# Loading three image pairs in one transfer each instead of two halves, in a sparse 3x3 convolution

## The chip, the cores and the metric

The kernel runs on one core of a Trainium2 chip. The metric is the device time of one execution in microseconds (us). Beside it stands the profile of one execution: its span runs from the first to the last instruction of the program, and it is a little shorter than the device time.

## The reference

The kernel computes a 3x3 convolution with zero padding of 1 over 16 images of 64 channels and 64x64 pixels, into 128 channels. Nine tenths of the weight's entries are zero, at random places; the kernel computes it densely.

```python
def reference(x, weight):          # x (16, 64, 64, 64), weight (128, 64, 3, 3), float32
    x_pad = np.pad(x, ((0, 0), (0, 0), (pad, pad), (pad, pad)), mode='constant')
    output = np.zeros((batch, c_out, h, w), dtype=np.float32)
    ...
                        if weight[co, ci, kh, kw] != 0:
                            output[b, co] += weight[co, ci, kh, kw] * x_pad[b, ci, kh:kh+h, kw:kw+w]
```

Input x is 16.8 MB, the output 33.6 MB, both float32 in HBM.

## The kernel before, in words

Two images make a pair: 2 x 64 channels fill the 128 partitions. There are eight pairs, p = 0 to 7. Each pair is worked on in four blocks of 16 output rows, so there are N = 32 blocks, k = 0 to 31, and block k belongs to pair k // 4. "The sixth, seventh and eighth pair" are p = 5, 6 and 7, and they are first used in blocks 20, 24 and 28.

For two output rows at a time the three row taps are folded into three products (five groups of matmuls, where plain work would take six). For each block GpSimd (POOL) makes `sums` (even rows plus odd rows, line 181) and `even` (a copy of the even rows, line 170), and ScalarE (ACT) makes `odd` (a copy of the odd rows, line 161). TensorE (PE) runs 30 matmuls on them (line 321). ACT copies the first product out of PSUM (line 276), and VectorE (DVE) adds it to the other two (lines 289 and 293) and so writes the output rows in SBUF. `sums`, `even` and `odd` have two buffers each, so POOL may be up to two blocks ahead: before it fills buffers for block k it waits until PE has done the products of block k-2 that read them (line 267).

Transfers go by two queues. SyncE's queue (SP, hardware descriptors, "q1 hardware_dynamic") loads the weight and the upper half of pair 0, and stores the output: pairs 0 to 5 in one transfer of 4 MB each (line 306), pairs 6 and 7 in two halves of 2 MB, the last half at line 355. A store is asked for when DVE has written its last row (a wait on `s_out`), and DVE may write an output buffer again four pairs later, once its store has landed (line 286). POOL's queue (software descriptors, "q0 software_dynamic") loads the images and casts them from float32 to bfloat16 on the way (line 103, in `load`): 1 MB are read and 0.5 MB written for a whole pair. Both queues feed the same 16 DMA engines.

When a load is asked for stands in two tables written out by hand. `PIECES[p]` (lines 39 to 43) lists the row ranges in which pair p is loaded; each piece has its own semaphore. `WHEN` (line 44) says behind which block's fills POOL asks for which piece. Pairs 0 to 3 are asked for before the loop over the blocks. Pair 4 comes in two pieces of 28 and 36 rows behind blocks 1 and 6. The loop on POOL is

```python
    for k in range(1, N):
        for fill_in, product in ((fill_sums, 2), (fill_even, 6)):
            if k >= UNROLL:
                wait(g, s_pe, 6 * (k - UNROLL) + product)
            fill_in(k)
        if k in WHEN:
            load(*WHEN[k])
```

A fill waits for every piece that holds one of its rows (`source`, lines 119 to 124). With halves, blocks 20, 24 and 28 need only the first half of their pair, and the next block already needs the second, since `even` reads one row beyond its 16.

Of the kernel before, what the change touches and what calls it, by code (L numbers as in the profile page):

```python
# [22 lines left out]
def kernel(  # L23
# [7 lines left out]
    B, C_IN, H, W = x.shape  # L31
# [7 lines left out]
    PIECES = {p: [(0, H)] for p in range(NP)}  # L39
    PIECES[0] = [(HEAD, H)]  # L40
    PIECES[4] = [(0, 28), (28, H)]
    for p in (5, 6, 7):
        PIECES[p] = [(0, H // 2), (H // 2, H)]
    WHEN = {1: (4, 0), 6: (4, 1), 8: (5, 0), 11: (5, 1), 14: (6, 0), 17: (6, 1), 20: (7, 0), 24: (7, 1)}

    def sbuf(name, shape, dtype):
        return nc.alloc_sbuf_tensor(name, shape, dtype).ap()
# [53 lines left out]
    def load(p, i=0):  # L101
        a, b = PIECES[p][i]
        nc.gpsimd.dma_start(out=xs[p][:, a:b, :], in_=pair(p)[:, a:b, :]).then_inc(s_x[p][i], 16)  # L103
# [160 lines left out]
# [8 lines that stand above are left out]
# [9 lines left out]
    for k in range(N):  # L281
        p, b = divmod(k, BLOCKS)
# [110 lines left out]
```

## Time and profile before

| | us |
|---|---|
| median of 3 runs | 126.63 |
| the runs | 125.82, 126.63, 131.43 |
| the profiled execution, its own device time | 126.62 |
| span of the profiled execution | 124.8 |
| PE busy in it | 110.0 |
| POOL busy in it | 64.3 |
| all 16 DMA engines together: packet time of both queues | 97.9% of the span |

The median and the profiled execution agree, so the profile stands for the median. Busy time of an engine counts its computing instructions; a DMA packet is one contiguous piece that one of the 16 DMA engines moves, and the share of a queue is the time of all its packets divided by 16 spans. Packets of one engine overlap slightly in the records, so a share of 102% in a stretch means full.

### The profile page before, as it was taken

The page shows a single profiled execution, that of the slowest core. Times are in us where ns is not written, and L with a number is a line of the kernel's source. Part 1 is how long each engine was busy: PE and PEld are TensorE (multiplying, and loading weights), DVE is VectorE, ACT ScalarE, POOL GpSimd, SP SyncE. Part 2 cuts the span into 40 slices and gives each one's busy share as a digit, 9 for nine tenths or more (in the row PEclk, how much of TensorE's full clock was granted, in tenths as well). Part 3 has the DMA queues.
Part 4 walks back from the last instruction along what each step waited for, and adds up shares of the span by engine and source line. Part 5 has one row for each costly group of instructions (what it writes and reads, how often), then busy time and mean ns, then how long its engine had stood idle before and what let it go on. Part 6 is the DMA issues. An engine that isn't in the chain of part 4 may idle for free.

```text
span 124.8 us, 2486 instructions
## 1 busy us (share of the span) xinstructions
PE 110.0 (88%) x983; PEld 56.5 (45%) x983; DVE 82.6 (66%) x74; ACT 54.5 (44%) x78; POOL 64.3 (52%) x89
## 2 busy tenths in 40 slices
PE   5979999999999999999999999999999999990000
PEld 1435555555555555555555555555555555540000
DVE  0576777777777777777777777777777777773000
ACT  4524555555555555554444444444444555530000
POOL 4469555575755755755675575557555555100000
PEclk9999999999999999999999999999999999999555
DMA  3999999999999999999999999999999999999990
GB/s 109 350 219 221 215 218 213 191 429 407 342 330 285 390 410 356 338 427 349 374 370 345 364 432 345 341 416 420 352 339 428 431 407 428 423 428 428 426 391 32
DMA packets 4739, 42.79 MB, mean 343 GB/s; under 512 B 384, under 2 KB 384, under 8 KB 1664
## 3 DMA queue, kind: packets, MB, share of 16 engines
q1 hardware_dynamic: 3008, 34.90, 66.9%
q0 software_dynamic: 1728, 7.87, 31.0%
q14 instruction: 3, 0.02, 0.0%
HBM read 17.07 MB, written 33.55 MB: 406 GB/s over the span
## 4 chain that ended last, share of the span: by engine, by line
PE 82%; DVE 2%; issue 0%; DVEq 0%
PE ps L321 82%; DVE home L293 1%; DVE home L289 1%; DVEq L144 0%
## 5 line engine op out<-in xcount | busy, mean ns | idle before, releaser
L276 ACT COPY pc<-ps 128x1024 f32<-128x1024 f32 x32 | 32.4, 1012 | 51.9 <-PE ps L321 51.9
L321 PE MATMUL ps<-odd,wT 64*128 64x504 bf16 (+1 forms) x384 | 47.2, 377 | 0.0
L321 PE MATMUL ps<-even,wT 64*128 64x504 bf16 (+1 forms) x384 | 47.2, 377 | 0.0
L289 DVE TENSOR_TENSOR o<-ps,pc 128x1024 f32<-128x1024 f32 x24 | 29.4, 1225 | 19.6 <-PE ps L321 19.6
L321 PEld LDWEIGHTS ps<-even,wT 64*128 64x128 bf16 x384 | 21.6, 94 | 19.9
L321 PEld LDWEIGHTS ps<-odd,wT 64*128 64x128 bf16 x384 | 21.6, 94 | 19.9
L293 DVE TENSOR_TENSOR o<-ps,pc 128x1024 f32<-128x1024 f32 x24 | 29.4, 1225 | 0.0
L321 PE MATMUL ps<-sums,wT 64*128 64x504 bf16 (+1 forms) x192 | 26.5, 377 | 0.7 <-PEq L332 0.7
L181 POOL TENSOR_TENSOR sums<-x 128x512 bf16<-128x512 bf16 x20 | 23.1, 1154 | 0.1
L170 POOL COPY even<-x 128x576 bf16<-128x576 bf16 (+1 forms) x20 | 13.0, 650 | 19.2 <-PE ps L321 19.2
L321 PEld LDWEIGHTS ps<-sums,wT 64*128 64x128 bf16 x192 | 10.7, 94 | 10.9 <-issue 1.2
L181 POOL TENSOR_TENSOR sums<-home 128x512 bf16<-128x512 bf16 (+1 forms) x11 | 13.3, 1212 | 2.8 <-DMA home<-in_x_dram 2.8
L289 DVE TENSOR_TENSOR home<-ps,pc 128x1024 f32<-128x1024 f32 x8 | 9.8, 1225 | 6.3 <-PE ps L321 6.3
L161 ACT COPY odd<-x 128x576 bf16<-128x576 bf16 (+1 forms) x20 | 13.2, 660 | 0.0
L170 POOL COPY even<-home 128x576 bf16<-128x576 bf16 (+2 forms) x11 | 6.7, 609 | 8.2 <-PE ps L321 8.0
L293 DVE TENSOR_TENSOR home<-ps,pc 128x1024 f32<-128x1024 f32 x8 | 9.8, 1225 | 0.0
L161 ACT COPY odd<-home 128x576 bf16<-128x576 bf16 (+1 forms) x10 | 6.6, 657 | 0.0
L171 POOL MEMSET even<- 128x64 bf16 x8 | 1.2, 151 | 10.3 <-PE ps L321 10.3
L237 PE MATMUL ps<-idle_rhs 128*128 128x512 bf16 x14 | 5.3, 538 | 1.4 <-DVE idle_rhs L202 1.4
L103 POOL DMA_DIRECT2D x<-in_x_dram x9 | 5.1, 565 | 0.0
L237 PEld LDWEIGHTS ps<-idle_rhs 128*128 128x128 bf16 x14 | 1.7, 129 | 3.7 <-issue 1.9
L198 DVE CAST w_bf<-w_sb 128x192 bf16<-128x192 f32 (+1 forms) x4 | 1.1, 352 | 2.4 <-DMA w_sb<-in_weight_dram 2.4
(21 smaller groups left out, 15.2 us busy)
## 6 DMA issues: line engine op xcount, KB each, us to landing
out_dram<-o SPq DMA_DIRECT2D x5, 4096.0 KB, 18.4
out_dram<-home SPq DMA_DIRECT2D x1, 4096.0 KB, 19.1
out_dram<-o SPq DMA_DIRECT2D x2, 2048.0 KB, 14.4
out_dram<-home SPq DMA_DIRECT2D x2, 2048.0 KB, 11.1
x<-in_x_dram POOLq DMA_DIRECT2D x6, 512.0 KB, 13.1
home<-in_x_dram POOLq DMA_DIRECT2D x2, 1024.0 KB, 13.5
home<-in_x_dram SPq DMA_DIRECT2D x1, 1024.0 KB, 5.9
x<-in_x_dram POOLq DMA_DIRECT2D x1, 1024.0 KB, 20.0
```

Of the source, the lines that this page charges most:

```text
L103: nc.gpsimd.dma_start(out=xs[p][:, a:b, :], in_=pair(p)[:, a:b, :]).then_inc(s_x[p][i], 16)
L161: copy or (lambda o, i: nc.scalar.copy(out=o, in_=i)),
L170: copy or (lambda o, i: nc.gpsimd.tensor_copy(out=o, in_=i)),
L171: zero or (lambda o: nc.gpsimd.memset(o, 0.0)),
L181: engine.tensor_tensor(out=sums[k % UNROLL], in0=src[:, r0 : r0 + ROWS : 2, :], in1=src[:, r0 + 1 : r0 + ROWS : 2, :], op=ADD,).then_inc(s ...
L198: copy(out=w_bf4[:, g, a:b, :], in_=w_v[:, k : k + b - a, :]).then_inc(done, 1)
L237: t.matmul(idle_ps, idle_rhs[:, 0:128], idle_rhs, start=True, stop=True)
L276: a.copy(out=pc[k % 3], in_=ps[0]).then_inc(s_pc, 1)
L289: v.tensor_tensor(out=o[:, :, r0 : r0 + ROWS : 2, :], in0=ps[1], in1=pc[k % 3], op=ADD).then_inc(s_free, 1)
L293: v.tensor_tensor(out=o[:, :, r0 + 1 : r0 + ROWS : 2, :], in0=ps[2 + k % 2], in1=pc[k % 3], op=ADD).then_inc(s_out, 1)
L321: mm = t.matmul(into[:, n, :, c_lo:c_hi], tap(g, kw, n), src[q, i : i + HALF, c_lo + kw - 1 : c_hi + kw - 1], start=(m == 0), stop=(m == l ...
```

## The change

```diff
     PIECES[4] = [(0, 28), (28, H)]
-    for p in (5, 6, 7):
-        PIECES[p] = [(0, H // 2), (H // 2, H)]
-    WHEN = {1: (4, 0), 6: (4, 1), 8: (5, 0), 11: (5, 1), 14: (6, 0), 17: (6, 1), 20: (7, 0), 24: (7, 1)}
+    WHEN = {1: (4, 0), 6: (4, 1), 8: (5, 0), 14: (6, 0), 21: (7, 0)}
```

Pairs 5, 6 and 7 keep the piece list that all pairs start with, `[(0, H)]`: one transfer with one semaphore. Pair 5 is asked for behind block 8 (its halves: blocks 8 and 11), pair 6 behind block 14 (14 and 17), pair 7 behind block 21 (20 and 24). The order of all computing instructions, and the stores, stay as they are. POOL issues three DMA instructions fewer, 9 instead of 12.

## The prediction

> **What bounds the kernel now.** I read the page first, then the chain of waits, then the table by stretches, then POOL's timeline. The page:
>
> ```profile
> PE 110.0 (88%) x983; PEld 56.5 (45%) x983; DVE 82.6 (66%) x74; ACT 54.5 (44%) x78; POOL 64.3 (52%) x89
> PE   5979999999999999999999999999999999990000
> DMA  3999999999999999999999999999999999999990
> DMA packets 4739, 42.79 MB, mean 343 GB/s; under 512 B 384, under 2 KB 384, under 8 KB 1664
> q1 hardware_dynamic: 3008, 34.90, 66.9%
> q0 software_dynamic: 1728, 7.87, 31.0%
> ```
>
> Two resources are full for nearly the whole span: PE until about 113 us, and the DMA engines from 3 us to the end. The two queues' packets fill 66.9 + 31.0 = 97.9% of 16 engines' span, 122.2 of 124.8 us. The chain of waits (start, length, what) names PE, but look where it ends:
>
> ```profile
> 8.28 102.64 PE ps L321 x948
> ...
> 112.24 1.23 DVE home L293
> ```
>
> DVE's last row is written at 113.47 us. The other 11.3 us of the span are the last store: SP's timeline has it (line 355) asked for at 113.76, and its 2 MB are 256 packets of 8 KB, 16 for each DMA engine at 309 ns (the trace's record of DMA packets), 4.9 us in all. So it waits and moves for 10.2 us (its time to landing) what takes 4.9. The table by stretches says why (stretch, length, PE, PEld, DVE, ACT, POOL busy, PE's clock, DMA share, GB/s):
>
> ```profile
> 48.00:60.00 12.00, 12.00 (x115) 6.27 (x112) 8.83 (x8) 6.42 (x9) 7.22 (x10) 1.00 1.02 369
> 72.00:84.00 12.00, 12.00 (x114) 6.28 (x112) 9.48 (x8) 5.45 (x8) 6.84 (x10) 1.00 1.03 386
> 108.00:114.00 6.00, 4.19 (x40) 1.93 (x35) 4.67 (x4) 1.01 (x1) 0.00 (x0) 1.00 1.01 427
> 114.00:118.00 4.00, 0.00 (x0) 0.00 (x0) 0.00 (x0) 0.00 (x0) 0.00 (x0) 0.69 1.01 426
> 118.00:122.00 4.00, 0.00 (x0) 0.00 (x0) 0.00 (x0) 0.00 (x0) 0.00 (x0) 0.50 0.88 371
> ```
>
> The DMA share is 1.00 or more in each stretch from 4 to 118 us. The last store queues behind earlier stores; its first packet moves at 116.7. **The DMA engines set the end, and they have no idle time before it**: the end comes when the sum of all packets is through, whatever their order. One engine finishes late, at 123.6, where the middle one of the 16 finishes at 121.7; the span ends on that one.
>
> How near is PE's path? The first store is asked for at 22.73 and its first packet moves at 25.0, 2.3 us later, with no store ahead of it. The last store could thus start at 113.76 + 2.3 = 116.1 instead of 116.7 (0.6 us of slack), and on the late engine, which starts it at 123.6 - 4.9 = 118.7, 2.6 us earlier. That is the most that the DMA work ahead can give; beyond it PE's pace (3.24 us a block) sets the end.
>
> **The change part by part.** *Packets removed.* Each half moves 128 packets that write 4096 bytes, one for each partition; a whole pair moves 128 of 8192. The packet records have 625 ns for the 8192-byte load packets (384 of them, pairs 1 to 3) and 324 ns for the 4096-byte ones (896, nearly all beside stores; median 322). Each transfer ends with 16 packets of 4 bytes, about 16 ns each. Before: 768 x 324.5 = 249.2 us of engine time for pairs 5 to 7; after: 384 x 625.2 = 240.1. Difference 9.1 / 16 = 0.57 us, and 48 closing packets fewer, 48 x 16 / 16 = 0.05 us. Sum: 0.62 us less DMA time. With the median of 322 for the small ones it is 0.45 + 0.05 = 0.50.
>
> Bounds: in a stretch in which only whole loads run, shares above 100% show that consecutive load packets overlap, so part of the cost of a packet may be hidden already. Two answers on the DMA queues, of 12:22 and of 46:54 us (packets, MB, share):
>
> ```profile
> q0 software_dynamic: 294, 2.15, 102.8%
> ```
>
> ```profile
> q1 hardware_dynamic: 159, 2.36, 70.1%
> q0 software_dynamic: 143, 0.52, 32.4%
> ```
>
> In the first, the 2.8% above full are 4.5 us over 262 load packets, 17 ns of overlap for each. In the second, with halves beside stores, the 2.5% are 3.2 us over some 128 load packets, up to 25 ns for each if all of it is theirs. The overlap is thus about as large as the 19 to 24 ns by which a packet is dearer, and if it came with every packet, small or large, the gain would be 0. Between 0 and 0.62 I take 0.5, near the packet times: store packets overlap too, so part of the second's 25 ns is theirs. Packet times and overlaps allow no more than 0.62, and a loss only if 8192-byte packets run slower beside stores than alone, which no row shows.
>
> *Closing cost of a transfer.* The Trainium skill (DMA: Bandwidth & Descriptors, "Anatomy of one DMA — SWDGE (gpsimd) path") puts about 2.0 us of fixed cost on each software-descriptor DMA; three fewer would give 6 us by that figure, as an estimate. The row speaks against it here: with other packets queued, the engines read 1.02 and 1.03 through the stretches in which halves close, so the fixed time is latency of one transfer and not idle engines.
>
> *Instructions on POOL.* DMA issues at blocks 11, 17, 20 and 24 go, one at 21 comes, 567 ns each: three fewer, 1.7 us of POOL time. POOL has idle time beside them (it waits 27.2 + 10.3 us for PE before `even`, 1.42 us in a block without an issue, 0.88 in one with), so this is worth nothing. The one added issue, at block 21, delays `sums` of block 22 from 74.03 to 74.6; the `even` behind it waits for PE until 76.61 anyway, and PE reads those sums some 5 us later. If that cover were gone, the cost would be 0.57 us. ACT and DVE issue nothing else; SP's queue is not touched, its stores are asked for at DVE's pace.
>
> *New waits.* Block 28 now needs all of pair 7, block 24 all of 6, block 20 all of 5. POOL's timeline (start, length, what):
>
> ```profile
> 73.37 0.66 POOL L170 COPY even<-x 128x576 bf16<-128x576 bf16 x1 [0.88 <-PE ps L321]
> ...
> 80.52 1.15 POOL L181 TENSOR_TENSOR sums<-x 128x512 bf16<-128x512 bf16 x1
> ...
> 93.48 1.15 POOL L181 TENSOR_TENSOR sums<-x 128x512 bf16<-128x512 bf16 x1
> ```
>
> The first row is `even` of block 21, so pair 7 is asked for at 74.03; the others are `sums` of blocks 24 and 28. Pair 7 must land by 93.48 for POOL not to wait, 19.4 us on. Behind that wait on POOL stand `even` of 28 and all later fills; PE reads `sums` of 28 at 99.04, so PE would wait only if the pair lands after 99.04 - 1.17 = 97.9, 23.8 us on (ACT's `odd` of 28 starts at 97.6). How long does a whole pair take beside stores? No row shows it. From below: a half takes 12.6 to 13.8 us. From above: pair 3, the one whole load behind two others, took 20.0, landing at 94.0, 0.5 late for POOL and early for PE. Between: a half's first packet moves 3.7 to 4.9 us after the issue, and its 8 packets per engine alternate with 16 KB store packets, 8 x (0.324 + 0.62) = 7.6 us, 12.3 of the 13.3 measured. Whole: 4.7 + 8 x (0.625 + 0.62) + 0.8 = 15.5 us. I take this; it lands at 89.5, 4 us before POOL's date. Cost 0. Pair 6 is asked for at 51.3 for 80.5, pair 5 at 31.8 for 67.5: 29 and 36 us ahead.
>
> *Order of DMA work.* The second halves of 5 and 6 move up by about 10 us, the first of 7 back by 3.3. Moving up only adds to the queue. Moving back could starve the engines at 71 to 76 us; but the store of pair 3 (asked for at 61.6, landing in 19.1 us) is still moving then, with about 5 us of packets left at 74, and pair 4's store is asked for at 74.6. So no idle time arises. Stores may land a few us later than now; pair 3's is asked for at 61.6, lands at 80.7, and DVE needs its buffer at block 28, after 99.0.
>
> Sum against the profiled execution: 126.62 - 0.5 = **126.1 us**; the 1.8 us outside the span stay. The median of the three runs, 126.63, is that execution's time.
>
> **The rivals.**
>
> *Packets already overlap.* All of the 19 to 24 ns of a packet is hidden, so nothing is gained: 126.6. For it: the 17 to 25 ns above. Against it: part of that overlap is that of store packets.
>
> *Slower: the whole pair 7 lands too late.* Place: POOL's wait ahead of `sums` of block 28. It decides from a landing of 97.9 on for PE, and for the end from 97.9 + 2.6 = 100.5 on, since the last store has that slack on the late engine. It would take engines that serve stores first: at 74 the store of 3 has 5 us left, that of 4 takes 256 x 611 ns / 16 = 9.8, that of 5 (asked for at 87.6) another 9.8, and then the pair 5.0: landing at 103.6. PE would be 103.6 + 1.2 - 99.0 = 5.8 late, the last store would start at 116.1 + 5.8 = 121.9 and end by 126.8, the span some 3 us later: 129.8. Against it: in 46:54 above both queues move at once, 70 to 32, and no load beside a store took over 13.8 us except the first piece of pair 4, queued behind others at 17.1. The Trainium skill (the same page, "Queues, rings and completion order") has the engines go round the queues packet by packet, which that row agrees with.
>
> *Faster than the packets say: a fixed cost of each transfer comes off the engines.* Three transfers at any cost over 0.9 us each would run into PE's path: at most 2.6 us, 124.0. Nothing in the stretches shows such idle time. The skill's 2.0 us, above, is the rule that would give it.
>
> *The change does nothing to the transfers*, because packets stay 4096 bytes: excluded nearly, since pairs 1 to 3 are loaded by the same call and have 8192.
>
> **How the numbers follow.** Forecast (0.3 to 0.9 us gained) 0.58; no gain, to within 0.3, 0.27; late pair 7, 0.05, of which a part costs under 2%; fixed cost comes off, 0.03; some other shift of a microsecond in the order of packets or in which engine ends last, 0.07. Runs of the same kernel differ by 0.8 us (125.82 and 126.63), and 2% (2.5 us) is about what a measurement of this kernel can tell from no change. The forecast's own range is 125.7 to 126.4; with the no-gain case and the scatter between runs it is 125.2 to 127.2. Faster by over 2%: 0.02; within 2%: 0.94; slower: 0.04.
>
> **What would show it.** Right: q0 with 1728 - 384 - 48 = 1296 packets and its share at (38.7 - 0.6) / 124.3 = 30.7%; packets under 8 KB down to 848; DMA share still 1.00 or more in all stretches from 4 to 118 us; PE without a new wait in front of blocks 20, 24, 28; whole loads landing in 15 to 17 us; DVE's last row still at 113.5, and the last store landing in about 9.7 us instead of 10.2. Wrong: a wait of POOL on pair 7 longer than 4 us, a stretch in the middle with a DMA share under 1, a whole load beside stores over 20 us, or load packets of 8192 bytes dearer than 644 ns beside stores: then the gain is a loss of as many ns x 24.

## The result, and the profile after

The changed kernel takes 126.65 us (median of 21 runs, 126.43 to 133.06), the kernel before 126.05 us beside it (21 runs, 125.75 to 131.95). The ratio is 1.0053, with a 95% interval of 1.004 to 1.0066; it leaves out the few executions of either kernel that took over 1.5% more than its fastest. The changed kernel is thus slower by about 0.65 us: little, but clear of the noise. The time lies inside the range of 125.2 to 127.2, but the forecast was a gain of 0.5 us, and the sign is wrong. That 126.65 also meets the 126.6 of the rival without gain is luck: both forecasts count from an execution of before that took 0.6 us more than that kernel's median.

The executions that were profiled cannot show it by their spans: the one of before took 126.62 us, and the one of after 126.55. A second profile of the kernel before (126.16 us) and two more of the changed one were therefore made; they are among the experiments.

The page of after:

```profile
PE 110.2 (88%) x983; PEld 57.3 (46%) x983; DVE 82.6 (66%) x74; ACT 54.6 (44%) x78; POOL 62.7 (50%) x86
DMA packets 4307, 42.79 MB, mean 343 GB/s; under 512 B 336, under 2 KB 336, under 8 KB 848
q1 hardware_dynamic: 3008, 34.90, 66.5%
q0 software_dynamic: 1296, 7.86, 30.9%
```

The load queue has exactly the 1296 packets foretold, 848 packets are under 8 KB, and both queues' shares have fallen: together 97.4% instead of 97.9%. The chain of waits and SP's timeline of after (start, length, what):

```profile
7.76 102.64 PE ps L319 x948
...
111.72 1.23 DVE home L291
```

```profile
113.24 0.37 SPq L353 DMA_DIRECT2D out_dram<-home  x1
```

In this execution TensorE began 0.5 us earlier and its stage is the same 102.64 us long, so no wait was added in front of any block. DVE's last row came at 112.95 instead of 113.47, and the last store was asked for 0.5 us earlier. The end did not follow: the store took 10.6 us to land instead of 10.2. The end belongs to the DMA engines, as the prediction said. POOL's timeline of after shows the loads' side:

```profile
73.45 0.57 POOL L101 DMA_DIRECT2D x<-in_x_dram  x1
74.04 1.16 POOL L179 TENSOR_TENSOR sums<-x 128x512 bf16<-128x512 bf16 x1
...
92.96 1.15 POOL L179 TENSOR_TENSOR sums<-x 128x512 bf16<-128x512 bf16 x1
```

Pair 7 was asked for at 73.45 and landed 14.4 us later, five us before `sums` of block 28 at 92.96, which did not wait. The table by stretches (columns as before):

```profile
48.00:60.00 12.00, 12.00 (x114) 6.36 (x112) 8.83 (x9) 5.96 (x9) 6.83 (x10) 1.00 1.00 382
72.00:84.00 12.00, 12.00 (x114) 6.34 (x112) 9.37 (x8) 5.56 (x7) 7.39 (x10) 1.00 1.01 354
108.00:114.00 6.00, 3.67 (x34) 1.72 (x30) 4.15 (x4) 1.01 (x1) 0.00 (x0) 1.00 1.01 427
114.00:118.00 4.00, 0.00 (x0) 0.00 (x0) 0.00 (x0) 0.00 (x0) 0.00 (x0) 0.72 1.01 428
118.00:122.00 4.00, 0.00 (x0) 0.00 (x0) 0.00 (x0) 0.00 (x0) 0.00 (x0) 0.50 0.85 360
```

The engines have no idle stretch here either (the lowest share of a stretch from 4 to 118 us is 0.99). So packet time went away, no engine idled, and the time rose. What differs is when loads move. Two answers on the DMA queues (packets, MB, share) for 66.2:74 us, before and then after:

```profile
q1 hardware_dynamic: 154, 2.51, 76.3%
q0 software_dynamic: 116, 0.41, 26.0%
```

```profile
q1 hardware_dynamic: 218, 3.31, 99.3%
```

Before, loads take a quarter of the engines in this stretch; after, none moves. A pair in halves took turns with the stores packet by packet for 16 x (0.303 + 0.608) = 14.6 us; a whole pair does so for 8 x (0.606 + 0.608) = 9.7 us. Counted in the packet records between 25 and 112 us, the time in which no load packet moves is 34.9 us before and 49.9 after.

And the stretch of 122.2:123.4 us on the DMA queues, before and then after:

```profile
q1 hardware_dynamic: 8, 0.05, 9.8%
```

```profile
q1 hardware_dynamic: 3, 0.02, 4.8%
```

One engine fully busy would be 6.25%. After, a single engine moves the last three packets; before, more than one is still moving. In both kernels the end is that of late engines, not of the sum over all.

### The profile page after: what moved, and what is told of

Its sections match the earlier page's. It is cut to its first block, busy times and chain, and to the rows that moved or that the text cites. A ratio compares the mean times of both kernels' runs of the same rounds, so it can differ in the third digit from the quotient of the medians.

```text
span 124.7 us, 2480 instructions
## 1 busy us (share of the span) xinstructions
PE 110.2 (88%) x983; PEld 57.3 (46%) x983; DVE 82.6 (66%) x74; ACT 54.6 (44%) x78; POOL 62.7 (50%) x86
## 3 DMA queue, kind: packets, MB, share of 16 engines
q0 software_dynamic: 1296, 7.86, 30.9%
## 4 chain that ended last, share of the span: by engine, by line
PE 87%; DVE 2%; issue 0%; DVEq 0%; SPq 0%
PE ps L319 82%; PE ps L235 4%; DVE home L291 1%; DVE home L287 1%; PE ps L239 1%; DVE idle_rhs L200 0%; DVEq L386 0%; DVEq L142 0%; SPq L90 0%
## 5 line engine op out<-in xcount | busy, mean ns | idle before, releaser
L101 POOL DMA_DIRECT2D x<-in_x_dram x6 | 3.4, 565 | 0.0
## 6 DMA issues: line engine op xcount, KB each, us to landing
x<-in_x_dram POOLq DMA_DIRECT2D x4, 1024.0 KB, 16.4
home<-in_x_dram POOLq DMA_DIRECT2D x2, 1024.0 KB, 12.9
home<-in_x_dram SPq DMA_DIRECT2D x1, 1024.0 KB, 5.4
```

## The experiments

Four theories were put to the runs. **S**: what differs is how late the slowest engine is. **P**: load packets of 8192 bytes cost the time as such. **O**: the dates and the bulk of the loads cost it. **M**, formed after the first four runs: one of the 16 engines falls behind whenever only stores move while TensorE runs, and hardly while loads move too; whole pairs get through sooner and leave more such time.

**The kernel before, again** (no edit).

> The kernel before, unchanged, for a second profile and as a control. Its first profiled execution (126.62 us) lies 0.6 us above the median of 21 runs (126.05), so a typical execution has not been seen. Every theory expects a ratio of 1.000 to within 0.002, and a span of about 124.1 us. What the profile should tell is where a typical execution is shorter than the one first shown: theory S (the end is set by how late the one slow DMA engine is) expects the last store's slowest engine nearer to the middle one than the 1.9 us of the first profile; theory P (packets) expects the middle engine's end earlier by about 0.6 us.

Ratio 1.0012 (0.9996 to 1.0028). The closing packets in the records give each engine's end, here and for the runs below (us from the span's start; "late engine" is the one that still loses time between 101 and 112 us, told as its distance from the middle one; a dash where it wasn't told apart):

```
run                   ratio   no load moves  middle engine  late engine  slowest
before (126.62 us)    -           34.9          121.56          +1.4      123.60
before again          1.0012      36.3          121.39          +1.5      123.15
eight turns           1.0021      35.6          121.37          +1.5      123.14
halves together       1.0029      36.4          121.64          +1.4      123.00
pair 5 in quarters    1.0009      31.2          121.63          +1.3      122.95
loads spread          0.9990      25.2          121.73          +1.3      122.99
pairs 5 and 6 whole   1.0033      47.1          121.28          +1.9      123.68
after                 1.0053      49.9          121.46          +2.0      123.43
after, third          1.0055      48.4          121.66          +2.0      123.63
8 KB stores           1.0068      50.6          121.99          +1.9      123.84
8 KB stores, whole    1.0085      56.1          122.41          +1.7      124.13
one tap, halves       1.0000      26.0          122.65           -        123.33
one tap, whole        0.9961      46.2          120.97           -        123.73
```

The profiled execution's device time is the slowest engine's end and 2.9 to 3.1 us in each row of the first eleven. Between before and after the middle engine hardly moves (121.4 to 121.7 in both); the late engine is 0.5 us later. This is what theory S says. It rests on telling the late engine apart: by the slowest engine alone the two kernels overlap (123.60 and 123.15, 123.43 and 123.63), because in both profiles of before another engine, which had lost its time earlier, was later still (+2.0, +1.8). Where no such engine is in the way, the late engine ends the kernel: its ends, 122.9 before and 123.4 to 123.6 after, and the 2.9 to 3.1 us give 125.8 to 126.0 and 126.3 to 126.7, close to the two medians of 126.05 and 126.65.

**The same dates, halves kept.**

```diff
+    WHEN = {1: [(4, 0)], 6: [(4, 1)], 8: [(5, 0), (5, 1)], 14: [(6, 0), (6, 1)], 21: [(7, 0), (7, 1)]}
...
+        for piece in WHEN.get(k, ()):
+            load(*piece)
```

> Pairs 5, 6 and 7 stay in halves, but both halves are asked for at once, behind blocks 8, 14 and 21: the dates of the changed kernel with the packets of the one before. Theory P (packets of 8192 bytes beside stores cost what was lost): same as before, ratio 1.000 to within 0.002. Theory O (the order of the DMA work, loads asked for in bulk, costs it): as the changed kernel, ratio 1.004 to 1.007.

Ratio 1.0029 (1.0003 to 1.0055), between the two; the run with eight turns below, whose transfers are those of before, gave 1.0021. The late engine is at +1.4, as before. The dates alone do not give the loss of the late engine. O falls for it; a small part of the time is within what these runs tell apart.

**Pair 7 alone, and pairs 5 and 6 alone, whole.**

> Only pair 7 loads whole, behind block 21; pairs 5 and 6 as before. Theory P: a third of the loss, ratio 1.002. Theory O with the cause near the end (pair 7's load is finished earlier, at 87 instead of 97 us): all of the loss, 1.005. Theory O with the cause earlier: 1.000.

> Pairs 5 and 6 load whole, behind blocks 8 and 14; pair 7 in halves as before. Theory P: two thirds of the loss, ratio 1.0035. Theory O with the cause at pair 7: 1.000; with the cause earlier: 1.005.

Ratios 1.002 (1.0002 to 1.0038) and 1.0033 (1.0005 to 1.006): about a third and two thirds of the loss, as it would be by P and, with 5 us of alternation less for each pair, by M. No single place holds it. (Of pair 7 alone only a long execution, 128.10 us, was profiled; it is not in the table.)

**What the late engine loses, and when.** The records do not number the engines, but each packet starts within some 20 ns of the end of the one before it on its engine, and so the late engine's packets were followed one by one in two profiles of after: the time in each stretch less the usual pitch of its packets (16 KB store 608 ns, 8 KB store 306, whole load 606). The table is its loss beyond that of the middle engine.

```
                         after                      after, third
loads move     29.4:46.9   0.03 us  0.002 per us     0.03 us   0.002
stores alone   46.9:55.4   0.36     0.043            0.38      0.043
loads move     55.4:65.6   0.01     0.001            0.04      0.004
stores alone   65.6:77.0   0.56     0.049            0.50      0.045
loads move     77.0:86.9   0.06     0.006            (other engines disturbed)
stores alone   86.9:98.0   0.51     0.046            0.49      0.047
stores alone   98.0:110    0.66     0.055            0.67      0.056
```

(The limits of the third profile's stretches differ by up to 0.7 us.) It loses only where no load moves, about 0.047 us per us. This is also what speaks most directly against P: while the 8192-byte load packets move, the engine loses almost nothing, and the middle engine's end did not move either. With 13.6 us more of such time (35 to 49), that is 0.64 us; the late engine's distance grew by 0.5, and the time by 0.65. From about 112 us on, with TensorE done, it loses nothing more in any profile.

**Longer alternation.**

```diff
+    PIECES[5] = [(16 * i, 16 * i + 16) for i in range(4)]
...
+    WHEN = {1: [(4, 0)], 6: [(4, 1)], 8: [(5, 0)], 9: [(5, 1)], 10: [(5, 2)], 11: [(5, 3)], 14: [(6, 0)], 17: [(6, 1)], 20: [(7, 0)], 23: [(7, 1)]}
```

> The kernel before, with pair 5 loaded in four quarters (16 rows each, behind blocks 8, 9, 10, 11) and pair 7's second half behind block 23. Theory M (one DMA engine loses about 0.055 us per us while only stores move, and almost nothing while loads and stores alternate; a pair alternates for 8 x (0.606 + 0.608) = 9.7 us whole, 16 x (0.303 + 0.608) = 14.6 in halves, 32 x (0.15 + 0.608) = 24.3 in quarters): 9.7 us more alternation, 0.5 us faster, ratio 0.996, at most as far as the next slowest engine lets it. Theory P (a cost of large load packets, absent in small ones): same as before, ratio 1.000, or a little slower by the closing packets. Theory O (bulk order): same as before.

```diff
+    PIECES[5] = [(16 * i, 16 * i + 16) for i in range(4)]
+    PIECES[6] = [(0, H // 2), (H // 2, H)]
+    PIECES[7] = [(0, 32), (32, 48), (48, H)]
+    WHEN = {1: [(4, 0)], 6: [(4, 1)], 8: [(5, 0)], 9: [(5, 1)], 10: [(5, 2)], 11: [(5, 3)], 14: [(6, 0)], 16: [(6, 1)], 20: [(7, 0)], 22: [(7, 1)], 25: [(7, 2)]}
```

> The kernel before with its loads spread over more of the time in which stores move: pair 5 in quarters behind blocks 8 to 11, pair 6 in halves behind 14 and 16, pair 7 as 32, 16 and 16 rows behind 20, 22 and 25. The run with pair 5 in quarters showed that what counts is not the alternation summed over pairs, as I had put it, but the time left in which no load packet moves: 31 us there against 35 before. Theory M in that form: some 21 to 24 us are left here, 12 less than before, the one engine is 0.6 us earlier, and the time falls until the next slowest engine ends it: ratio 0.996 to 0.999. Theory P: 1.000. If it isn't below 1.000 though the time without loads falls and the one engine's lag too, another engine sets the end.

Ratios 1.0009 (0.9986 to 1.0032) and 0.999 (0.9956 to 1.0023). The first was a miss: I had added up alternation over the pairs, though loads in the kernel before already follow each other closely, so only 4 to 5 us were gained. The second was a miss for M's size: only 25 us are left without loads, but the late engine, which should have been 0.6 us earlier, still ends at +1.3, since 0.6 us of its loss lie behind 97 us, after the last load. The next engines end at 122.6 and 122.9, close to its 123.0. No version here beats the kernel before beyond the interval.

**Smaller store packets, with halves and with whole pairs.** Each store of pairs 0 to 5 becomes two transfers of 32 rows, asked for together.

```diff
-        parts = 2 if p in HALVED else 1
+        parts = 2
...
-            s.wait_ge(s_out, BLOCKS * p + BLOCKS // parts * (h + 1))
+            s.wait_ge(s_out, BLOCKS * p + (BLOCKS // parts * (h + 1) if p in HALVED else BLOCKS))
```

> The kernel before, its loads untouched; the stores of pairs 0 to 5 are asked for at the same time as before, but as two transfers of 32 rows, so that their packets have 8 KB instead of 16. Load packets then alternate with 306 ns store packets instead of 608, so loads get through sooner: a pair in halves alternates for 16 x (0.303 + 0.306) = 9.7 us instead of 14.6, as a whole pair did beside 16 KB packets. Theory M: slower by 0.055 x (3 x 4.9 + 2.4 for pair 4) = 0.9 us, ratio 1.007. Theory P (load packets): 1.000, or up to 1.001 for 96 more closing packets on 16 engines.

> The changed kernel (pairs 5 to 7 whole) with the 8 KB store packets of the run before: a whole pair then alternates for 8 x (0.606 + 0.306) = 7.3 us instead of 9.7. Theory M: the time without load packets grows by about 3 x 2.4 + 2.4 to some 59 us, 24 more than before; at 0.055 that is 1.3 us, ratio 1.009 to 1.010, at most some 0.4 us above either change alone. Theory P (a cost of large load packets, and another of small store packets, both in full): 0.65 + 0.85 us, ratio 1.012.

Ratios 1.0068 (1.0045 to 1.0091) and 1.0085 (1.0057 to 1.0114). With untouched loads the time without loads rose to 50.6 us and the kernel lost as much as M said; but that is only half M. The table shows the middle engine 0.4 to 0.6 us later as well: two 8 KB packets take 2 x 306 = 612 ns against 608, 96 times on each engine, 0.4 us. The late engine's own part is +0.4. With whole pairs its distance is +1.7, less than after's +2.0 though still more time is without loads: a miss for M's size. Why its middle engine ends another 0.4 us later (122.41) is open.

**What the one engine loses time to.** Four kernels changed the number of matmuls or TensorE's loop: one column tap of three, two of three, a loop of eight turns, and none.

```diff
-KW_ORDER = (1, 0, 2)
+KW_ORDER = (1,)
```

> For the cause of the one engine's loss only: two of the three column taps are left out of all products (10 matmuls a block instead of 30), so TensorE issues a third of its instructions; the loads and stores stay. The output lacks those taps. If the loss comes with TensorE's instruction stream, the one engine loses about a third as much in a stretch in which only stores move (0.2 us in 10 instead of 0.55). If it comes with the stores or with the engine itself, it loses 0.5 as before. The end is then still set by the DMA engines, near 122 us.

> For the cause of the one engine's loss: one of the three column taps is left out (20 matmuls a block instead of 30; the output lacks that tap). With one tap the loss was gone while TensorE still ran, though only about 5 us of that lay in a stretch without loads. If each TensorE instruction costs the one engine its share, some 0.35 to 0.45 us are lost in 10 us without loads; if the loss starts only where the loop's body is longer than some length, it is either 0 or near 0.55.

> The kernel before, with TensorE's loop of 16 turns over two blocks made into 8 turns over four; the same matmuls in the same order. It asks what the one engine's loss comes from. If it is the instructions themselves (each turn's instructions are brought in again by this one engine), as many are brought in per us: the loss stays 0.055 us per us in a stretch without loads, and the time 1.000 to within 0.002. If it is something once a turn, the loss halves (0.27 us in 10), and the time falls until another engine ends it: 0.997 to 0.999.

> The kernel before, with TensorE's loop written out in full, so that no turn jumps back; the same matmuls in the same order. Instructions brought in by the one engine: as many, loss 0.055 and time 1.000, with instruction packets now seen in the DMA records, or else spread over other engines. Something once a turn: the loss is gone, and the time falls to what the next engine sets, 0.995 to 0.999.

Each of the first two was run once. With one tap (125.77 us) only stores move from 88 us on, and TensorE's last matmul ends at 93.9. The stretch 88.3:91.7:

```profile
88.30:91.70 3.40, 3.00 (x14) 0.94 (x14) 1.49 (x2) 1.41 (x3) 3.40 (x6) 0.50 0.98 419
```

Until 92.2 us no engine loses anything, though TensorE is busy; its granted clock is 0.50 here. From 91.8 us on the clock is back at 1.00, and one engine loses 0.1 us between 92.3 and 94.2. With two taps (126.16 us) TensorE works without loads until 92.7 us:

```profile
86.00:93.00 7.00, 6.32 (x56) 2.65 (x52) 6.47 (x6) 2.60 (x3) 3.41 (x5) 1.00 1.00 428
```

One engine is late by 13 to 42 ns with each of 11 store packets in a row here, 0.36 us in 7: 0.05 us per us, as with all taps. With eight turns (1.0021, 0.9979 to 1.0063) the late engine loses the same 0.5 us as with sixteen, so it is nothing that comes once a turn. Without a loop (1.002, 0.9995 to 1.0046) instruction packets appear:

```profile
q8 instruction: 7, 0.11, 0.3%
```

Seven of 16 KB, each taking some engine about 0.9 us, and still one engine falls behind by 0.27 us within each of two 4.9 us stretches. Jumping back is thus not the cause either. What the taps have to do with the loss is taken up at the last pair of runs.

**Two store queues.** The changed kernel, with image two of each store of pairs 0 to 5 on ScalarE's queue, and a control with both images on SP's.

```diff
+        if k % BLOCKS == 0 and 0 < k // BLOCKS <= 6:
+            store_image(a, k // BLOCKS - 1, 1)
```

> The changed kernel with its loads untouched (pairs 5 to 7 whole, same dates); of each store of pairs 0 to 5 image one goes by SP's queue and image two by ScalarE's (asked for behind the first block of the next pair), so that each DMA engine has two store queues and one load queue to take turns with. Packets keep their sizes (16 KB). A whole pair should then alternate for 8 x (0.606 + 2 x 0.608) = 14.6 us, as two halves did before, instead of 9.7. Theory M: the time without load packets falls from 50 back to some 35 us, the one engine's lag on the middle one from 2.0 to 1.4 or 1.5 us, and the loss is gone: ratio 1.000 to 1.002. Theory P (8192-byte load packets cost it): as the changed kernel, 1.004 to 1.007.

> The control to the run with two store queues: the same two transfers for each store, image by image, but both by SP's queue. Every theory expects the changed kernel's time, ratio 1.004 to 1.007, with 96 closing packets more (0.05 us), some 50 us without load packets and a lag of about 2 us.

Ratios 1.0083 (1.0055 to 1.0112) and 1.0089 (1.0053 to 1.0125). The time without loads fell only to 44.5 us (50.4 in the control). M would then give a lag 0.3 us smaller; measured were 1.93 and 1.94 us, a miss for M. The pair decides little all the same: the profiled executions took 127.84 and 127.80 us, 0.9 more than their medians, and the first has a gap of its own. Its table by stretches:

```profile
36.00:40.00 4.00, 4.00 (x42) 2.08 (x38) 3.21 (x3) 1.83 (x3) 2.57 (x4) 1.00 0.86 148
```

The engines are not full there (0.86). Its middle engine ends at 122.8, but so does the control's (122.7), in which no stretch of 4 us from 4 to 112 us falls below 0.97; why that one is late is open.

**The changed kernel, again.**

> The changed kernel unchanged, for a second profile beside the second one of the kernel before. Theory M: the one engine sets the end again, 1.9 to 2.0 us behind the middle one, with some 50 us without load packets; ratio 1.004 to 1.007. If its lag is near 1.5 as in the kernel before, M falls.

> The changed kernel once more, since its second profile was of a long execution (128.07 us, its slowest engine 3.4 us behind the middle one, against 2.0 in the first). Theory M expects a typical execution near 126.6 us to show its slowest engine 1.9 to 2.0 us behind the middle one and the middle one at 121.4 to 121.5 us, as in the kernel before.

Ratios 1.0061 (1.0035 to 1.0087) and 1.0055 (1.0042 to 1.0067). The second profile was of a long execution (128.07 us): one engine ended 3.4 us behind the middle one, and at the closing of the store near 92 us it was already 2.4 behind (0.9 in the first profile). The third (126.75 us) is typical, with the middle engine at 121.66 and the late one at +1.96.

**Halves against whole pairs, with little for TensorE to do.** One tap of three, with the loads of before and with those of after.

> Loads of the kernel before (halves), with two of three column taps left out of all products (10 matmuls a block, output without those taps), timed. With a single time of 125.77 us and a lag of 0.4 us of the slowest engine in the first look, 125.8 us are expected, ratio 0.998 to 1.000. It is the base for the run beside it, with whole pairs.

> The changed kernel's loads (pairs 5 to 7 whole) with the same two taps left out. Theory M (the one engine falls behind while only stores move and TensorE is running; with a third of the matmuls it hardly does): the same time as the halves beside it, to within 0.2 us, and a lag of the slowest engine of 0.4 to 0.7 us. Theory P (load packets of 8192 bytes cost 0.65 us as such, whatever TensorE does): 0.65 us over the halves beside it, ratio 0.005 higher.

Ratios 1.000 (0.998 to 1.0019) and 0.9961 (0.9947 to 0.9975): with whole pairs the kernel is 0.5 us *faster* than with halves. M had expected the same time to within 0.2 us and a lag of 0.4 to 0.7; the slowest engine of the second profile is 2.8 us late, 1.9 of which it had lost in the first 10 us, and that execution took 126.65 us, 1.15 more than its kernel's median. Both are misses. P had expected 0.65 us more, and that is wrong too, but this pair alone does not refute it: TensorE waits for loads in both kernels, and the middle engines differ by 1.7 us in the two profiles, which is open.

What the pair does show is when an engine loses time. Two stretches of the second, in both of which only stores move:

```profile
75.00:81.00 6.00, 4.09 (x20) 1.29 (x20) 5.34 (x5) 1.58 (x2) 1.82 (x3) 0.50 1.01 431
81.50:92.20 10.70, 7.35 (x50) 2.46 (x48) 10.54 (x11) 7.44 (x10) 5.79 (x8) 0.94 1.00 429
```

In the first no engine loses more than 0.01 us. In the second, between the closings of two stores (81.7 to 82.5 and 91.4 to 92.3 us, and the slowest engine 2 us later), 15 engines keep their distances to within 0.002 us and one, not the last, falls back by 0.445. That is 0.044 us per us, within the full kernel's range, with 50 matmuls in 10.7 us where the full kernel issues some 100. It ends with TensorE's last matmul at 92.1 us, while DVE works on until 94.4. **In these profiles the loss does not shrink with the number of matmuls.** In the kernels with one tap it appears where the granted clock is at or near 1.00 and is absent at 0.50 (here, in the stretch 88.3:91.7 above, and in 87.4:91.5 of the halves); in the full kernel the clock stays at 1.00 until 115 us, and the loss ends with the matmuls at 112. That the clock decides is not shown, since no run set it alone.

## Why the prediction was wrong

- **"The end comes when the sum of all packets is through, whatever their order."** This step failed. It holds for the middle engine, 121.4 to 121.7 in both kernels. The span ends with one late engine, and that engine's lag does depend on the order: it loses 0.047 us per us while only stores move and TensorE runs. The prediction saw a late engine (123.6 against 121.7; the closings put the middle one at 121.6) and took its lag as given.
- **"Packets removed": 0.5.** The term was mis-sized; it measured 0, to within the 0.2 us by which the middle engine's end scatters (121.56 and 121.39 before, 121.46 and 121.66 after). The sum of packet times fell as worked out, from 122.2 us per engine (before again) to 121.6 (after). But a load packet's successor starts 19 ns before its end, a store packet's 3 ns before; so the pitch is 303 ns for 4096 bytes and 606 for 8192, and two small ones cost what a large one does. With 24 load packets fewer on each engine, 24 x 19 = 0.46 us of overlap went with them. (Store packets beside loads last 624 ns instead of 611, and after has some 14 fewer of these on each engine; these 0.2 us do not show in the middle engine's end either.) The rival "packets already overlap" (chance 0.27) was the right one for this term: its 17 to 25 ns were there to be read, and I let the store packets explain part of it away.
- **Closing cost of a transfer.** Right: three transfers fewer took no idle time off the engines. The Trainium skill (DMA: Bandwidth & Descriptors, "Rules for kernel authors") advises transfers of 1 MiB and more for bandwidth. That is what the change made of 0.5 MB transfers; the middle engine's end did not move here, so with the queues always full the trace does not bear it out. (A whole pair reads 2 MB and writes 1 MB, as the profile's 1024.0 KB for a load has it; the 1 MB and 0.5 MB given with the kernel before are those of a half.)
- **New waits, POOL's instructions.** Right: no wait at blocks 20, 24, 28. Landings of 16.5, 16.2 and 14.4 us against 15 to 17 foretold (the last a little under), POOL 1.6 us less busy to no effect.
- **Order of DMA work.** Half right: no engine idled. But "no idle time" was read as "no cost".
- **The slower rival.** A late pair 7 did not happen. The mechanism that did make it slower was none of the rivals that were worked out; it falls under the remainder of 0.07 ("in which engine ends last"), which named no cause and no direction.
- **The base.** The profiled execution stood for the median of three runs; of 21 runs the median was 0.6 us lower, as large as the effect. And 2% was not the least that can be told apart: the interval here is 0.13% either way.

What is shown: that one late engine ends the kernel, that it loses its time in the stretches without loads, and that it loses almost none while the 8192-byte load packets move. Argued from rates: that 13.6 us more of such stretches make the whole 0.65 us; the two profiles give 0.5 for the late engine, and the runs that lengthened the alternation or split the store queue did not give the gains that the rate foretold. Open: why this one engine, and what it has to do with TensorE; neither the number of matmuls nor the loop's turns change it.

## What to carry to other kernels

When DMA queues are full to the end, look at each engine's last packet, not only at the sum: the latest of 16 sets the end, and what it lost here depended on which queues moved beside each other. Merging transfers saved packets in the records here but no time, since consecutive packets overlap; compare pitches, not durations. To tell whether an engine lost time, follow its packets or compare all 16 closings as a set: sorted by time, engines change places, and a loss of 0.4 us by one that is not the last hides among them. For effects under 1%, have several executions profiled before one is taken for typical.

## What the runs showed of the hardware

One DMA engine of 16 fell behind by 0.043 to 0.056 us per us while only stores moved and TensorE ran at full rate, and by 0.001 to 0.006 while loads moved too. Loop turns (16, 8, none) made no difference to it, and neither did half as many matmuls per us (0.044 in the kernel with one tap); in that kernel it was absent in the stretches in which the granted clock was 0.50. Load packets overlap with their successor by 19 ns, store packets by 3 ns. TensorE's loop written out in full brought seven 16 KB instruction packets into the span, each about 0.9 us on one engine.
